# A build-time list scheduler is told that transfers land later, rotary tables load later, and the input ring grows from seven slots to eight

## The chip, the cores and the metric

The program runs on one core of a Trainium2 chip. The metric is the device time of one execution in microseconds, the median over the runs. The engines are called PE (matmul), DVE, ACT and POOL (elementwise work) and SP, which here only issues transfers. PE runs in order, and so does each other engine; they wait for each other by semaphores.

## The reference

One decoder layer on x of 1024 rows by 1024 columns, all in float32:

```
h = rmsnorm(x) * gain
p = h @ w_in                       # 1696 columns for the RWKV mixer, 1536 for attention
r, k, v, wd, ad, gd = split(token_shift_mix(p[:, :1696]))
g = sigmoid(gd) @ g_lora_up;  a = sigmoid(a0 + ad @ a_lora_up);  decay from tanh(wd) @ w_lora_up
y_rwkv = group_norm(scan of the 64x64 state of each of 8 heads) + bonus, times g
q, k, v = split(p[:, 1696:]);  rotary on the first 16 of 64 dims
y_attn = three dilated causal windows (128,1) (512,4) (2048,16), merged, normed
x = x + concat(y_rwkv, y_attn) @ w_out
gate, val = split(rmsnorm(x) @ w_ffn_up);  gate = causal conv of width 3
x = x + (silu(gate) * val) @ w_ffn_down
out = rmsnorm(x)
```

## The kernel before

Nothing in the kernel is ordered by hand. Each piece of work is handed to a scheduler that runs while the program is built (`Plan`): an op has the engines that may do it with an estimated cost on each, a rank, and the ops and buffers that it waits for. The scheduler keeps a clock of its own for each engine, takes the ready op with the best rank, and writes it down; the order in which it wrote the ops of an engine is the order in which the chip runs them. A transfer gets a `lag`, the time that its bytes take, and the scheduler holds its users back until a landing time:

```
            if eng == "SP":
                self.moved = max(self.moved, self.free[eng] + 0.6) + o.lag
                o.end = self.moved + 0.9
```

So a landing time or a lag moves no transfer by itself: it changes the moment from which a user counts as ready, and with it what is written ahead of what on every engine from there on. Nearly all transfers are issued by SP, in one queue.

The stages, with the times of the profiled execution: the first norm of x, in four groups of 256 rows (0 to 42 us); the dense input projection (to about 220 us); the RWKV mixer in 8 units (`keys`, inverses, state steps) with twelve attention column tiles at0 to at11 of the projection between them as filler for PE (220 to 490); attention heads (490 to 670); the output projection (580 to 745); the second norm (690 to 757); a Strassen-form up projection and convolution (759 to 1168); the down projection (1200 to 1404).

In the start, x comes in as 8 tiles x_0 to x_7 of 128 rows. Each is squared and summed (L370, ACT), scaled (L376, DVE), transposed in 128x128 pieces on PE (`pt_n`, L386), and copied out as a rounded high part `hT_hi` (L292 on ACT or L294 on DVE) and the rest `hT_lo` (L395, DVE). `x_n` is a ring of buffers for the x tiles and `jk_n` a ring for the squares. The gate columns `gd` and the columns `wa` of the projection are worked on as the groups come. `grow_d` (L337) writes 1024 gain values, one by one, to DRAM. `lwr` and `glr` are the two up matrices of the low-rank gates, which ACT casts to `lwh` and `gl`.

For each projected tile `in_proj` splits weights and h into two rounded parts and runs three products (L475 to L477): hi by hi, lo by hi, hi by lo. Its `cut` says in how many pieces a half of 512 rows is worked. For a unit q of the mixer, `keys` loads BK, AR and v, PE makes `pbk` (L854), `pgm` (L802) and `pv` (L839) of them, the masked products go through DRAM (`md`) into `mk`, DVE inverts 32x32 blocks (L888, L894), which come back through `mdo` into `inv`, and PE uses `inv` in `pd` (L925). In attention `kv` and `qd` read back what the tiles stored in `qkv_d`; `pav` (L1178) and `psc` (L1206) are the first products of a head. In the second norm, DVE makes `jk_n` (L1474) and PE transposes it (L1489); `a11l` (L301) is the low part of the first up-projection weights, made from the loads `rg` and `rv`.

Of the kernel before, what the change touches and what calls it, by code (L numbers as in the profile page):

```python
# [18 lines left out]
P = 128  # L19
S = 1024  # L20
D = 1024
# [58 lines left out]
class Plan:  # L80
# [70 lines left out]
    def run(self, until=None):  # L151

        until = list(until) if until is not None else None
        while any(self.todo.values()):
# [34 lines left out]
            if eng == "SP":  # L189
                self.moved = max(self.moved, self.free[eng] + 0.6) + o.lag  # L190
                o.end = self.moved + 0.9
            for u in o.users:
# [12 lines left out]
def planned_layer(ctx: ExitStack, tc: tile.TileContext, a, out):  # L205
# [14 lines left out]
    def ring(tag, n, shape, pool, dtype=F32):  # L220
        plan.ring(tag, n)
        if pool.space == PSUM:
            plan.banks.add(tag)

        def new(name):
            return plan.buf(tag, lambda: pool.tile(shape, dtype, tag=tag, name=name, bufs=n))

        return new
# [55 lines left out]
    def copy(eng, out, in_):  # L284
        if eng == ACT:
            nc.scalar.copy(out, in_)
        else:
            nc.vector.tensor_copy(out, in_)  # L288
# [38 lines left out]
    def derived():  # L327
# [8 lines left out]
        {SP: 0.5},  # L336
        lambda: nc.sync.dma_start(out=grow_d.rearrange("o (k p) -> p (o k)", p=P), in_=par[:, g_ : g_ + KD]), -150, [par_in],  # L337
        lag=1.0,
# [80 lines left out]
    with tc.tile_pool(name="xp", bufs=1) as xp:  # L419
        x_n, jk_n = ring("x", 7, [P, D], xp), ring("xjk", 1, [P, D], xp)  # L420
        for g in range(4):
# [16 lines left out]
        def in_proj(cols, name, R, evacuate, after=None, Rw=None, twice=False, cut=1):  # L438
# [16 lines left out]
            def wide():  # L455
                return raw.t[:, :, None, :r].broadcast_to([P, KD, 2, r]) if twice else raw.t[:, :, :r]

            def parted(t):
                return t[:, :, :m].rearrange("p k (x c) -> p k x c", c=r) if twice else t[:, :, :m]

            Rw = max(Rw, -279.5)
            o = chain["w"] = plan.op(COPY, lambda eng: copy(eng, parted(hi.t), wide()), Rw, ins, [raw, hi, lo])
            o2 = plan.op(
                pool(2.3), lambda: lower(POOL, parted(lo.t), wide(), parted(hi.t)), Rw, [o], [raw, hi, lo]
            )
# [77 lines left out]
        zg = tmp_n("zg")  # L543
        z_in = in_proj([(1600, GCOLS)], "gd", -198, shift_mix(13, lambda: zg.t, -198, "gd", [zg]), None, -288.5)
        gr = slice(0, GCOLS)
# [232 lines left out]
    def unit(q):  # L778
# [6 lines left out]
                b, lambda b=b: b.t.rearrange("p (f c) a t -> p f (c a t)", f=NFT),  # L785
                lambda src=src: src[:, :, q2].rearrange("f p t -> p f t"), 1.5, RB,
            )
            for b, src in ((bk, bk_d), (ar, ar_d))
        ]
        vload = load(vt, lambda: vt.t, lambda: v_d[:, :, qs].rearrange("f p t -> p f t"), 0.8, RB)  # L790

# [31 lines left out]
        def g3():  # L823
# [5 lines left out]
        stored = [  # L829
            load(gm, lambda b=b: md[b].rearrange("q s t -> s q t"), lambda b=b: g3()[blocks[b], :, blocks[b]], 0.4, RC, masked)  # L830
            for b in range(2)
# [36 lines left out]
        for rs in rss:  # L868
            o = load(mk, lambda rs=rs: mk.t[rs], lambda: md.rearrange("b q s t -> (b q) s t"), 0.4, RC, stored)
            copies.append(o)  # L870
# [29 lines left out]
        for r in range(4):  # L900
            o = plan.op(
                pool(0.06), lambda r=r: nc.gpsimd.memset(mp.t[rss[r]].rearrange("p s t -> p (s t)")[:, r : 256 : 36], 1.0),
                RC, prev, [mp],
            )
            back.append(load(mp, lambda r=r: dealt[r], lambda r=r: mp.t[rss[r]], 0.18, RC, [o]))
        inv = inv_n(f"inv{q}")
# [191 lines left out]
    for half_ in range(2):  # L1098
        tsl = slice(half_ * 512, half_ * 512 + 512)
        tabs = [rope_n(f"rope{half_}_{i}") for i in range(2)]  # L1100
        tabs_in = [
            load(tabs[i], lambda i=i, tabs=tabs: tabs[i].t, lambda i=i, tsl=tsl: a["rope"][:, i, tsl], 1.0, 200 + 5, (), tabs)
            for i in range(2)
# [811 lines left out]
```

## Time and profile before

| | us |
|---|---|
| median of 3 runs | 1426.93 (1420.82, 1426.93, 1427.86) |
| the profiled execution | 1429.69, of which its span is 1427.5 |
| PE busy | 1365.1 (96%) |
| DVE busy | 999.3 (70%) |
| ACT busy | 554.4 |
| POOL busy | 340.8 |

The span is what the trace covers; the execution's own time is 2.19 us longer. The profiled execution took 2.76 us more than the median.

### The profile page before, as it was taken

To read this page: it belongs to the slowest core of one execution; us is meant where nothing else is said; L and a number is where in the kernel's file an instruction comes from. 1 tells how busy PE (TensorE), PEld (TensorE's weight loads), DVE (VectorE), ACT (ScalarE), POOL (GpSimd) and SP (SyncE) were. 2 spreads that over 40 slices of the span, in tenths; PEclk is the share of its full clock that TensorE was granted. 3 is DMA by queue.
4 is the path that set the end of the run, shared out by engine and by line. 5 is a ranking of instruction groups with operands and counts; after the bars stand their busy time and mean duration, and the time that the engine had idled before them with its cause. 6 is when DMAs were issued, how large, how long until landed. Compare 5 with 4: busy or idle time off the path is not lost.

```text
span 1427.5 us, 21004 instructions
## 1 busy us (share of the span) xinstructions
PE 1365.1 (96%) x7872; PEld 1129.4 (79%) x7872; DVE 999.3 (70%) x2020; ACT 554.4 (39%) x957; POOL 340.8 (24%) x366
## 2 busy tenths in 40 slices
PE   5999999999999889999989999999999999999997
PEld 4788887787788777888767888888888887888886
DVE  5566663867878378988589777777777757565547
ACT  5433332133222368776245434433333434222213
POOL 4223223143453357652231000000000005111101
PEclk9999999999999989999999999999999999999999
DMA  6143437545654446522743222222222237322203
GB/s 183 45 135 119 144 111 255 155 119 161 169 148 110 105 121 188 168 85 89 247 142 102 89 89 75 74 89 86 77 89 89 78 131 248 118 89 89 89 30 118
DMA packets 172565, 173.02 MB, mean 121 GB/s; under 512 B 39632, under 2 KB 142416, under 8 KB 171440
## 3 DMA queue, kind: packets, MB, share of 16 engines
q1 hardware_dynamic: 172320, 171.16, 39.4%
q8 instruction: 62, 1.02, 0.3%
q10 hardware_dynamic: 144, 0.52, 0.1%
q14 instruction: 39, 0.32, 0.1%
HBM read 119.22 MB, written 52.43 MB: 120 GB/s over the span
## 4 chain that ended last, share of the span: by engine, by line
PE 76%; DVE 11%; DMA 7%; ACT 1%; issue 1%; POOL 1%; SPq 1%; DVEq 0%; POOLq 0%; ACTq 0%
PE c L1554 29%; PE pd L1754 5%; PE pd L1752 5%; PE pd L1753 5%; PE po L1268 2%; PE pb_at L475 2%; DVE it L888 2%; PE po L1402 2%; PE po L1403 2%; PE po L1401 2%; PE ppt L1238 1%; DVE mp L894 1%; PE pb_at L477 1%; PE pb_at L476 1%; DMA mk<-md 1%
## 5 line engine op out<-in xcount | busy, mean ns | idle before, releaser
L301 POOL TENSOR_TENSOR wl<-rw,wh 128x512 fp32r<-128x512 f32 x22 | 32.8, 1496 | 558.0 <-ACT wh L1439 544.4
L1760 DVE TENSOR_TENSOR dx<-dx,pd 128x512 f32<-128x512 f32 x128 | 85.9, 684 | 86.4 <-PE pd L1754 85.8
L1754 PE MATMUL pd<-wl,ah 128*128 128x512 f32 x352 | 138.4, 393 | 2.8 <-POOL wl L301 2.8
L1752 PE MATMUL pd<-wh,ah 128*128 128x512 f32 x352 | 138.1, 392 | 0.2 <-DVE dx L288 0.2
L1753 PE MATMUL pd<-wh,al 128*128 128x512 f32 x352 | 138.1, 392 | 0.1
L1625 DVE TENSOR_TENSOR uval<-uval,c 128x512 f32<-128x512 f32 x67 | 45.9, 685 | 62.5 <-PE c L1554 62.3
L475 PE MATMUL pb_at<-hT_hi,wh_at 128*128 128x512 f32 x192 | 82.5, 430 | 0.0
L1754 PEld LDWEIGHTS pd<-wl,ah 128*128 128x128 f32 x352 | 66.7, 190 | 17.2 <-POOL wl L301 3.2
L1752 PEld LDWEIGHTS pd<-wh,ah 128*128 128x128 f32 x352 | 66.8, 190 | 14.6 <-DVE dx L288 0.6
L1753 PEld LDWEIGHTS pd<-wh,al 128*128 128x128 f32 x352 | 66.7, 189 | 14.6 <-POOL al L301 0.5
L477 PE MATMUL pb_at<-hT_hi,wl_at 128*128 128x512 f32 x192 | 76.3, 397 | 0.0
L476 PE MATMUL pb_at<-hT_lo,wh_at 128*128 128x512 f32 x192 | 76.2, 397 | 0.0
L1656 DVE SCALAR_TENSOR_TENSOR uga<-ug,par,uga 128x1023 f32<-128x1023 f32 (+1 forms) x44 | 56.4, 1281 | 15.8 <-ACT uga L1650 15.8
L888 DVE TENSOR_TENSOR it<-mk,mp 128x60 f32<-128x60 f32 (+19 forms) x240 | 64.0, 284 | 3.3
L894 DVE TENSOR_TENSOR mp<-mp,it 128x60 f32<-128x60 f32 (+20 forms) x240 | 54.5, 244 | 3.4
L1554 PE MATMUL c<-T,s1h 128*128 128x512 f32 x176 | 55.0, 393 | 1.0 <-DVE T L1498 1.0
L1554 PE MATMUL c<-B,a11h 128*128 128x512 f32 x176 | 54.9, 392 | 0.7 <-DVE B L1498 0.5
L1554 PE MATMUL c<-B,a12h 128*128 128x512 f32 x176 | 54.7, 392 | 0.7 <-ACT uval L1629 0.7
L1554 PE MATMUL c<-T,a22h 128*128 128x512 f32 x176 | 54.8, 393 | 0.0
L1554 PE MATMUL c<-B,s4h 128*128 128x512 f32 x176 | 54.8, 393 | 0.0
L1554 PE MATMUL c<-T,s3h 128*128 128x512 f32 x176 | 54.8, 393 | 0.0
L1554 PE MATMUL c<-T,s2h 128*128 128x512 f32 x176 | 54.8, 393 | 0.0
(335 smaller groups left out, 3722.0 us busy)
## 6 DMA issues: line engine op xcount, KB each, us to landing
rg<-in_w_up SPq DMA_DIRECT2D x22, 512.0 KB
rv<-in_w_up SPq DMA_DIRECT2D x22, 512.0 KB
ra<-act_d SPq DMA_DIRECT2D x22, 512.0 KB
rw<-in_w_down SPq DMA_DIRECT2D x22, 512.0 KB
act_d<-uga SPq DMA_DIRECT2D x21, 512.0 KB
x<-in_x SPq DMA_DIRECT2D x16, 512.0 KB
wr_at<-in_w_in SPq DMA_DIRECT2D x12, 512.0 KB
qkv_d<-spl SPq DMA_DIRECT2D x24, 256.0 KB
```

Source lines behind the costliest of these rows:

```text
L475: nc.tensor.matmul(acc.t[:m, cs], hi.t[:, k, :m], hT_hi[k][:, ts_], start=(k == 0), stop=False)
L476: nc.tensor.matmul(acc.t[:m, cs], hi.t[:, k, :m], hT_lo[k][:, ts_], start=False, stop=False)
L477: nc.tensor.matmul(acc.t[:m, cs], lo.t[:, k, :m], hT_hi[k][:, ts_], start=False, stop=(k == KD - 1))
L888: nc.vector.tensor_tensor(t3(), mk.t[:, k : k + 1, k + 1 :].broadcast_to([P, r, n]), mp.t[:, 0:r, k : k + 1].broadcast_to([P, r, n]), ALU. ...
L894: nc.vector.tensor_tensor(mp.t[:, 0:r, k + 1 :], mp.t[:, 0:r, k + 1 :], t3(), ALU.add)
L1554: nc.tensor.matmul(bank.t, w.t[:, js], m, start=start and j == 0 and s, stop=j == 3 and w is lo, skip_group_check=True,)
L1625: {DVE: 0.69}, lambda: nc.vector.tensor_tensor(half_of(*out_), half_of(*x_), four(bank), ALU.add), R, after,
L1656: lambda x=x: nc.vector.scalar_tensor_tensor(ga.t[:, x:], g.t[:, : S - x], pc(f"cw{2 - x}", f), ga.t[:, x:], ALU.mult, ALU.add),
L1752: nc.tensor.matmul(pd.t, ah.t[:, ts_], wh.t, start=(j == 0), stop=False)
L1753: nc.tensor.matmul(pd.t, al.t[:, ts_], wh.t, start=False, stop=False)
L1754: nc.tensor.matmul(pd.t, ah.t[:, ts_], wl.t, start=False, stop=(j == n_ - 1))
L1760: lambda i=i, sl=sl, pd=pd: nc.vector.tensor_add(xr[i].t[:, sl], xr[i].t[:, sl], pd.t), R,
```

## The change

Seven edits. The scheduler's landing time of a transfer goes from 0.9 to 1.6 after its bytes. The lags of the mixer's transfers in short rows go up (BK and AR 1.5 to 1.9, v 0.8 to 1.2, `md` 0.4 to 0.8, `mk` 0.4 to 0.6, `mdo` 0.18 to 0.4). The store of `grow_d` gets a later rank. The x ring has eight slots and the ring of squares two. The low part of the weights of a `cut` projection may be made by POOL or DVE, where POOL alone made it. The `gd` projection is cut in two pieces of 256 rows. The rotary tables are loaded only after two attention column tiles (`cols_out[1]`).

```diff
             if eng == "SP":
                 self.moved = max(self.moved, self.free[eng] + 0.6) + o.lag
-                o.end = self.moved + 0.9
+                o.end = self.moved + 1.6
...
-        lambda: nc.sync.dma_start(out=grow_d.rearrange("o (k p) -> p (o k)", p=P), in_=par[:, g_ : g_ + KD]), -150, [par_in],
+        lambda: nc.sync.dma_start(out=grow_d.rearrange("o (k p) -> p (o k)", p=P), in_=par[:, g_ : g_ + KD]), 60, [par_in],
         lag=1.0,
...
-        x_n, jk_n = ring("x", 7, [P, D], xp), ring("xjk", 1, [P, D], xp)
+        x_n, jk_n = ring("x", 8, [P, D], xp), ring("xjk", 2, [P, D], xp)
...
+            how = LOW if cut > 1 else pool(2.3)
             o2 = plan.op(
-                pool(2.3), lambda: lower(POOL, parted(lo.t), wide(), parted(hi.t)), Rw, [o], [raw, hi, lo]
+                how, lambda *eng: lower(*(eng or (POOL,)), parted(lo.t), wide(), parted(hi.t)), Rw, [o], [raw, hi, lo]
             )
...
-        z_in = in_proj([(1600, GCOLS)], "gd", -198, shift_mix(13, lambda: zg.t, -198, "gd", [zg]), None, -288.5)
+        z_in = in_proj([(1600, GCOLS)], "gd", -198, shift_mix(13, lambda: zg.t, -198, "gd", [zg]), None, -288.5, False, 2)
...
-                lambda src=src: src[:, :, q2].rearrange("f p t -> p f t"), 1.5, RB,
+                lambda src=src: src[:, :, q2].rearrange("f p t -> p f t"), 1.9, RB,
...
-        vload = load(vt, lambda: vt.t, lambda: v_d[:, :, qs].rearrange("f p t -> p f t"), 0.8, RB)
+        vload = load(vt, lambda: vt.t, lambda: v_d[:, :, qs].rearrange("f p t -> p f t"), 1.2, RB)
...
-            load(tabs[i], lambda i=i, tabs=tabs: tabs[i].t, lambda i=i, tsl=tsl: a["rope"][:, i, tsl], 1.0, 200 + 5, (), tabs)
+            load(tabs[i], lambda i=i, tabs=tabs: tabs[i].t, lambda i=i, tsl=tsl: a["rope"][:, i, tsl], 1.0, 200 + 5, cols_out[1], tabs)
```

The diff shows what the scheduler is told; what it makes of that stands in the order of the instructions. Three places follow (a name's last number counts buffers, and is another one in the changed kernel; its line numbers from L464 on are one higher).

The first is SP's queue in the start, from the seventh x tile to the first weights of the k columns. Before:

```order
L304 DMA x_6_162<-in_x 128x1024
L304 DMA wr_gd_175<-in_w_in 128x8x96
L337 DMA grow_d_85<-par_69 128x8x1
L304 DMA x_7_235<-in_x 128x1024
L308 DMA cst2_117<-in_consts2 128x384
L304 DMA lwr_310<-in_wa_lora 128x1024
L304 DMA glr_320<-in_g_lora 96x512
L304 DMA wr_k0_527<-in_w_in 128x8x128
```

And in the changed kernel:

```order
L304 DMA x_6_162<-in_x 128x1024
L304 DMA x_7_164<-in_x 128x1024
L304 DMA wr_gd_177<-in_w_in 128x8x96
L337 DMA grow_d_85<-par_69 128x8x1
L308 DMA cst2_117<-in_consts2 128x384
L304 DMA lwr_274<-in_wa_lora 128x1024
L304 DMA glr_284<-in_g_lora 96x512
L304 DMA wr_k0_551<-in_w_in 128x8x128
```

The last x tile has moved ahead of the gate columns' weights and of `grow_d`; the rest stands as it stood, and `grow_d` still stands ahead of `cst2`, `lwr` and `glr`. On ACT, before, the square of x_7 stood between copies of the second group, and the two casts of the low-rank matrices ahead of seven of the eight copies of the third:

```order
L292 ACTIVATE hT_hi6_101<-pt_n1_1_6_302,par_69 128x256
L370 ACTIVATE jk_n1_3_1_323,ss_n1_3_1_135<-x_7_235 128x1024
L292 ACTIVATE hT_hi7_102<-pt_n1_1_7_312,par_69 128x256
L286 CAST lwh_139<-lwr_310 128x1024
L286 CAST gl_143<-glr_320 96x512
L292 ACTIVATE hT_hi1_96<-pt_n1_2_1_363,par_69 128x256
```

In the changed kernel:

```order
L292 ACTIVATE hT_hi6_101<-pt_n1_1_6_303,par_69 128x256
L292 ACTIVATE hT_hi7_102<-pt_n1_1_7_311,par_69 128x256
L286 CAST lwh_139<-lwr_274 128x1024
L286 CAST gl_143<-glr_284 96x512
L292 ACTIVATE hT_hi0_95<-pt_n1_2_0_365,par_69 128x256
L292 ACTIVATE hT_hi1_96<-pt_n1_2_1_368,par_69 128x256
```

The square of x_7 is gone from here (it stands four rows above the first one shown), and the two casts stand ahead of all eight copies of the third group.

The second place is PE at the first unit of the mixer, from the first product of its keys to `pv0`. `pb_at1_0` are filler matmuls of an attention column tile. Before (rows that only repeat are left out; a `pgm` pair has eight rows, of which the last stands here):

```order
L477 MATMUL pb_at1_0_1825<-hT_hi4_99,wl_at1_1719 128x512
L854 MATMUL pbk0_0_1857<-cst_68,BK0_1816 128x128 x4
L854 MATMUL pbk0_1_1864<-cst_68,BK0_1816 128x128 x4
L475 MATMUL pb_at1_0_1825<-hT_hi5_100,wh_at1_1718 128x512
...
L802 MATMUL pgm0_0_1_1874<-AR0_1818,BK0_1816 128x128
L839 MATMUL pv0_1885<-cst_68,v0_1823 128x128 x4
L475 MATMUL pb_at1_0_1825<-hT_hi6_101,wh_at1_1718 128x512
...
L802 MATMUL pgm0_1_1_1898<-AR0_1818,BK0_1816 128x128
```

In the changed kernel:

```order
L478 MATMUL pb_at1_0_1849<-hT_hi6_101,wl_at1_1747 128x512
L855 MATMUL pbk0_0_1880<-cst_68,BK0_1840 128x128 x4
L855 MATMUL pbk0_1_1886<-cst_68,BK0_1840 128x128 x4
L476 MATMUL pb_at1_0_1849<-hT_hi7_102,wh_at1_1746 128x512
...
L803 MATMUL pgm0_0_1_1896<-AR0_1842,BK0_1840 128x128
L476 MATMUL pb_at1_1_1910<-hT_hi0_95,wh_at1_1746 128x512
...
L803 MATMUL pgm0_1_1_1916<-AR0_1842,BK0_1840 128x128
L840 MATMUL pv0_1926<-cst_68,v0_1847 128x128 x4
```

Six filler matmuls (the pieces 5 and 6 of the tile, three each) have moved ahead of `pbk0`, and `pv0` now stands behind the second `pgm` pair and the three filler matmuls ahead of it.

The third place is PE after the last filler matmul of the last column tile, up to the first head of attention. Before:

```order
L477 MATMUL pb_at11_1_4596<-hT_hi7_102,wl_at11_4368 128x512
L960 MATMUL pzu_1776<-state1_1781,AR7_3967 128x128 x4
L969 MATMUL pzu_1776<-UV7_4056,Gm7_4060 64x64 x8
L982 MATMUL pzu_1776<-zs0_1778,Gm7_4060 64x64 x8
L992 MATMUL pzs_1777<-UV7_4056,BKt7_4042 64x64 x8
L1035 MATMUL pzu_1776<-UV7_4056,Gm7_4060 64x64 x8
L1178 MATMUL pav0_4824<-cst_68,kv0_4783 128x64 x8
```

In the changed kernel:

```order
L478 MATMUL pb_at11_1_4494<-hT_hi7_102,wl_at11_4225 128x512
L970 MATMUL pzu_1800<-UV6_3801,Gm6_3811 64x64 x8
L1072 MATMUL pyt5_4637<-cst_68,Y5_4429 128x128 x4
L983 MATMUL pzu_1800<-zs0_1802,Gm6_3811 64x64 x8
L993 MATMUL pzs_1801<-UV6_3801,BKt6_3795 64x64 x8
...
L932 MATMUL pd7_4699<-Gm7_4085,inv7_4630 32x32 x16
L983 MATMUL pzu_1800<-zs1_1803,Gm6_3811 64x64 x8
L1179 MATMUL pav0_4775<-cst_68,kv0_4692 128x64 x8
```

Ten pieces of mixer work now stand between the end of the last tile and `pav0`, where five stood; the unit in hand at that point is the seventh (q = 6), where it was the eighth.

## Rows read from the trace of the kernel before

**Rows 1.** The page: busy time by engine, and the chain that ended last.
```profile
PE 1365.1 (96%) x7872; PEld 1129.4 (79%) x7872; DVE 999.3 (70%) x2020; ACT 554.4 (39%) x957; POOL 340.8 (24%) x366
...
PE 76%; DVE 11%; DMA 7%; ACT 1%; issue 1%; POOL 1%; SPq 1%; DVEq 0%; POOLq 0%; ACTq 0%
```

**Rows 2.** Waits of PE: what for, us in total, times, longest us.
```profile
PE pt_n L386 <- DVE x L376: 10.6, 2, 7.2
...
PE pd L925 <- DVE inv L910: 4.4, 3, 3.4
PE pav L1178 <- DMA kv<-qkv_d: 3.4, 1, 3.4
...
PE pt_n L1489 <- DVE jk_n L1474: 3.1, 3, 2.2
...
PE pv L839 <- DMA v<-v_d: 1.7, 1, 1.7
...
PE pbk L854 <- DMA BK<-bk_d: 1.2, 1, 1.2
```

**Rows 3.** The chain in the start: from us, us, what.
```profile
14.98 11.82 DMA x<-in_x
```

**Rows 4.** SP's issues in the start: from us, us, what.
```profile
10.24 0.38 SPq L337 DMA_DIRECT2D grow_d<-par  x1
...
15.86 0.42 SPq L304 DMA_DIRECT2D lwr<-in_wa_lora  x1
```

**Rows 5.** Stretches of 2 us: busy by engine, clock, DMA share, GB/s.
```profile
20.00:22.00 2.00, 2.00 (x19) 2.00 (x18) 1.84 (x5) 0.71 (x2) 0.91 (x1) 1.00 0.18 33
...
26.00:28.00 2.00, 0.00 (x0) 0.00 (x0) 0.00 (x0) 1.12 (x3) 0.00 (x0) 0.50 1.08 336
```

**Rows 6.** ACT from 24 to 43: from us, us, what [idle before].
```profile
29.02 1.05 ACT L286 CAST lwh<-lwr 128x1024 fp32r<-128x1024 f32 x1 [0.63 <-DMA lwr<-in_wa_lora]
29.97 0.61 ACT L286 CAST gl<-glr 96x512 fp32r<-96x512 f32 x1
```

**Rows 7.** DVE from 24 to 43, same columns.
```profile
28.83 4.23 DVE L376 TENSOR_SCALAR x<-x,rs_n 128x1024 f32<-128x1024 f32 x3
...
34.68 4.00 DVE L395 SCALAR_TENSOR_TENSOR hT_lo<-pt_n,par,hT_hi 128x256 fp32r<-128x256 f32 x10
...
41.34 0.74 DVE L496 SCALAR_TENSOR_TENSOR zwa<-pb_wa,par,zwa 128x511 f32<-128x511 f32 x1
```

**Rows 8.** PE at 42 us, the end of the start, same columns.
```profile
42.29 0.47 PE L475 MATMUL pb_wa<-hT_hi,wh_wa 128*128 128x512 f32 x1 [1.38 <-DVE carry_wa L504]
```

**Rows 9.** Stretches of 8 us, columns as rows 5.
```profile
224.00:232.00 8.00, 5.13 (x38) 3.88 (x37) 1.29 (x2) 1.07 (x2) 4.90 (x8) 1.00 0.86 273
...
280.00:288.00 8.00, 6.76 (x71) 5.53 (x72) 5.62 (x22) 1.03 (x2) 1.31 (x1) 0.61 0.80 180
...
488.00:496.00 8.00, 3.55 (x57) 3.21 (x58) 2.17 (x4) 3.57 (x6) 5.49 (x5) 1.00 1.01 258
...
696.00:704.00 8.00, 5.78 (x30) 4.66 (x29) 5.22 (x6) 2.67 (x6) 1.94 (x4) 1.00 0.86 278
```

**Rows 10.** PE at the first unit, columns as rows 6.
```profile
225.60 0.39 PE L476 MATMUL pb_at<-hT_lo,wh_at 128*128 128x512 f32 x1
225.83 0.39 PE L477 MATMUL pb_at<-hT_hi,wl_at 128*128 128x512 f32 x1
...
229.08 1.16 PE L802 MATMUL pgm<-AR,BK 64*128 64x128 f32 x16
```

**Rows 11.** SP's issue of the rotary tables.
```profile
228.65 5.36 SPq L304 DMA_DIRECT2D rope<-in_rope  x4
```

**Rows 12.** The chain into attention.
```profile
489.00 6.16 DMA kv<-qkv_d
```

**Rows 13.** DVE at the second norm, columns as rows 6.
```profile
698.93 0.69 DVE L301 TENSOR_TENSOR a11l<-rg,a11h 128x512 fp32r<-128x512 f32 x1 [0.76 <-DMA rv<-in_w_up]
699.54 2.30 DVE L1474 SCALAR_TENSOR_TENSOR jk_n<-x,rs_n,grow 128x1024 f32<-128x1024 f32 x1
```

More of the change, by code (lines that the diff above doesn't have):

```diff
@@ L829, in unit @@
         stored = [
-            load(gm, lambda b=b: md[b].rearrange("q s t -> s q t"), lambda b=b: g3()[blocks[b], :, blocks[b]], 0.4, RC, masked)
+            load(gm, lambda b=b: md[b].rearrange("q s t -> s q t"), lambda b=b: g3()[blocks[b], :, blocks[b]], 0.8, RC, masked)
             for b in range(2)
@@ L868, in unit @@
         for rs in rss:
-            o = load(mk, lambda rs=rs: mk.t[rs], lambda: md.rearrange("b q s t -> (b q) s t"), 0.4, RC, stored)
+            o = load(mk, lambda rs=rs: mk.t[rs], lambda: md.rearrange("b q s t -> (b q) s t"), 0.6, RC, stored)
             copies.append(o)
@@ L904, in unit @@
             )
-            back.append(load(mp, lambda r=r: dealt[r], lambda r=r: mp.t[rss[r]], 0.18, RC, [o]))
+            back.append(load(mp, lambda r=r: dealt[r], lambda r=r: mp.t[rss[r]], 0.4, RC, [o]))
         inv = inv_n(f"inv{q}")
```

## The prediction

> **What bounds the kernel now.** I read the page first: PE is busy for 1365.1 of 1427.5 us, and the chain that ended last runs through PE for 76%, through DVE for 11% and through transfers for 7% [rows 1]. The change leaves PE's work as it was but for 24 longer matmuls cut in two, so it can only win or lose in the 62.4 us in which PE stands still, and where PE runs at its lower clock after standing still. The second view is therefore the list of PE's waits: 10.6 us for scaled x in the start, 4.4 for the inverses, 3.4 for the first `kv` of attention, 3.1 for the second norm, 1.7 and 1.2 for v and BK of the first unit [rows 2]. The third is each of these places by itself: the chain and the queues of the start [rows 3 to 8], and the stretches of 8 us in which PE's idle time lies [rows 9]. A place gains only where something else than the moved transfer ends the wait next, so I ask that each time.
>
> **The start.** The chain goes from x_7's issue at 14.98 for 11.82 us to its landing at 26.8 [rows 3]. It was issued late, since a ring of seven made it wait for x_0, and it then moved slowly: `grow_d`, issued at 10.24 [rows 4], was still being written in pieces of four bytes. From 20 to 22 us only 33 GB/s moved, against 336 from 26 to 28 with the store gone [rows 5]. With eight slots x_7 stands ahead of `grow_d` and should land at about 15. That takes the 4.23 us of late scaling on DVE [rows 7] out of the way. The new rank of `grow_d` does not take it out from ahead of `cst2`, `lwr` and `glr`; the order shows that it stays there.
>
> What is late next is `lwr`. Before, ACT got it at 29.02 and was through with `lwh` and `gl` 1.56 us later (29.97 plus 0.61), at 30.58 [rows 6]. After, the half megabyte of x_7 is no longer between `grow_d` and `lwr`, at 336 GB/s some 1.6 us, so that ACT is free at 29.0. Behind the two casts stand all eight copies of the third group, and then the fourth. Then 16 `hT_lo` and two `hT_hi` at 0.40 us each (4.00 for ten [rows 7]) take 7.2 us, and the shift mix and what follows it 0.95 (41.34 to PE's start at 42.29 [rows 7, 8]). Dense work starts at 29.0 + 8.15 = 37.15, against 42.29: 5.1 us earlier. I take 0.6 off, since the low-rank products now stand ahead of the first k tile and have little slack behind their sigmoid and tanh: **4.5 us gained**. The bounds: nothing, if the store holds `lwr` as long as it held x_7 and the casts end where they did with copies then waiting as before; 7.2, if `lwr` is not held at all, which is the longest of PE's waits for scaled x, gone whole [rows 2].
>
> One rule bears on what is held. By the rows, transfers behind `grow_d` crawl until it is written (33 GB/s). The Trainium skill, "DMA: Bandwidth & Descriptors", section "Queues, rings and completion order", says that descriptors are consumed in ring order on each engine, but that data descriptors carry no barrier and a later one may finish its write before an earlier one. By the second half of that rule `lwr` would land before the store is done, and the start would gain 7.2 where I say 4.5; by the row, it would not. The row decides here, as the transfer held in it was of the same size in the same queue.
>
> **The cut of gd and the low weights on DVE.** Long matmuls follow each other 0.23 us apart, and 16 of a quarter of the columns take 1.16 in all, 0.07 each [rows 10]. So two half-length ones cost 0.14 to 0.23 against 0.23; I take nothing, with an upper bound of 24 x 0.23 = 5.5 us, which would need the shorter matmul to be no shorter at all. The two low parts on DVE are worth one to three microseconds there, in the time that the late scaling leaves free.
>
> **The first unit of the mixer.** From 224 to 232 PE is busy for 5.13 of 8 us [rows 9], and the two waits, 1.2 for BK and 1.7 for v, are the whole of it [rows 2]. The scheduler now thinks that they land later, and so six filler matmuls stand ahead of `pbk0` (6 x 0.23 = 1.4, over 1.2), and 1.16 of `pgm` with three more (0.7) ahead of `pv0` (together 1.9, over 1.7) [rows 10]. **2.9 gained**, both covered by little; the bounds are 0 (the loads move later by as much) and 2.9.
>
> **The inverses.** Before, the four rotary tables keep SP busy for 5.36 us from 228.65 [rows 11], ahead of the first unit's `md` and `mk`; after, they come later, and `mk` lands sooner. Against that, the weights of at4 are now copied on DVE behind the first inversion, and `pd` of later units stands earlier in PE's order. The wait here was 4.4 in three [rows 2], and from 280 to 288 PE also ran at 0.61 of its clock [rows 9]. I take **nothing**, between 5 gained (this wait and some of the clock) and 5 lost.
>
> **Into attention.** The `kv` load takes 6.16 us from 489.00 [rows 12] and PE waits 3.4 of that [rows 2]; PE is busy for 3.55 of 8 us in this stretch [rows 9]. In the new order five more pieces of mixer work, each of 16 small matmuls at around 1 us (1.16 for a `pgm` group [rows 10]), stand between the last column tile and `pav0`: some 5 us, over 3.4. What is late next is the first `psc`, which waits for POOL's half of the keys, so I take **3 gained** with bounds of 0 and 4.45, the idle of that stretch. Inside attention DVE has little room, and I take nothing there, 4 either way.
>
> **The second norm.** `a11l` stands ahead of `jk_n` on DVE and waits for a weight load (0.76), though `jk_n` needs none of it, and PE waits 2.2 for `jk_n` [rows 2, 13]. After, `jk_n` stands ahead of `a11l`, and DVE has two splits less to do there (they went to other engines). **2 gained** of the 2.22 idle in that stretch (8 less 5.78 [rows 9]). The bounds are 0 and 2.2. The rest of the program keeps its order at the places where PE waits: nothing.
>
> **The sum** is 4.5 + 2.9 + 0 + 3 + 2 = 12.4. From the profiled execution's 1429.69 that gives 1417.3; that execution stands 2.76 above the median of the runs, 1426.93, so the forecast for the median is **1414.5**.
>
> **The rivals.** *All of the start*: `lwr` is not held, and the start gains 7.2 in place of 4.5: 1414.5 - 2.7 = **1411.8**. For it: x_7's late issue alone explains most of 26.8; against it, the 33 GB/s with x_7 waiting. *The estimates change little*: the waits at the first unit, at attention and in the second norm only move, since a load that is thought to land later is not issued sooner, and the slot freed in one place is filled by the next late thing. Only the start is left: 1426.93 - 4.5 = **1422.4**. For it: each of these waits is covered by only 0.2 us or so, and DVE is nearly full in attention. *Inverses too early in PE's order* (slower): `pd` of the third and fifth units stand 52 and 33 long matmuls earlier on PE than before, while nothing makes DVE's inverses faster. If DVE keeps its times, PE waits 52 x 0.23 + 33 x 0.23 = 19.6 us, and loses each time what it lost from 280 to 288 at a clock of 0.61, 0.39 x 8 = 3.1: 25.8 in all, against 12.4: **1440.3**. It decides from the point where the inverses lag by more than 12.4 us together. Against it: `mk` is no longer behind the rotary tables, and DVE was idle for over 2 of 8 us there [rows 9].
>
> **How the numbers follow.** My forecast gets 0.50, the whole start 0.13, the start alone 0.25, the inverses 0.12. About 0.5% (7 us) is what a measurement of this kernel can tell from no change, which makes faster anything under 1419.8 and slower anything over 1434.1. Of my forecast nine tenths lie under 1419.8, with all of the second case and a fifth of the third: 0.45 + 0.13 + 0.05 = 0.63. The same gets 0.05 + 0.20 = 0.25, slower 0.12. The forecast's own range is 1409 to 1420, from the bounds of its terms; with the cases the range reaches from 1406 (the first rival, with 5 gained at the inverses) to 1428 (the third with some new waits), which leaves out the slower case and little else.
>
> **What would show it.** Right, if in the profile of the changed kernel dense PE work starts at 36 to 39 us, x_7 lands at about 15, ACT's cast of `lwh` is what ends a wait at 27 to 28; if PE waits for neither BK nor v at 224 to 232, nor over 1 us for `kv`; and if `jk_n` of the second norm ends ahead of `a11l`. Wrong, if a wait for `inv`, `mk` or the copy of at4's weights on DVE grows past 5 us between 250 and 450, if PE's idle in attention grows, or if the start ends at 42 again because the store holds `lwr`.

## The result, and the profile after

The changed kernel takes 1408.66 us (median of four runs, 1405.70 to 1410.13) against 1426.93 us. The medians differ by 18.3 us where 12.4 was forecast. The ratio on record, formed over the runs, is 0.9883 with a 95% interval of 0.9861 to 0.9905, which is 13.6 to 19.8 us: faster, and by more than the forecast. The time lies within the range on record and 0.3 us below the forecast's own range.

The page of the changed kernel, with the rows that answer to [rows 1]:

```profile
span 1407.9 us, 21049 instructions
...
PE 1356.3 (96%) x7896; PEld 1126.9 (80%) x7896; DVE 989.6 (70%) x2021; ACT 553.5 (39%) x961; POOL 326.5 (23%) x361
...
PE 80%; DVE 9%; DMA 6%; ACT 1%; SPq 1%; issue 1%; POOL 1%; DVEq 0%; POOLq 0%; ACTq 0%
```

PE does the same work with 24 more instructions, and yet is busy for 8.8 us less. That part is the clock: matmuls that ran at the lower of its two levels (1.2 GHz, 0.50 in the rows) ran at the higher one (2.4 GHz, 1.00). So the gain is to be looked for in two sums, PE's idle time and what it lost to a low clock. I worked both out in steps of 2 us from the trace: idle is 2 less PE's busy time, and slow is the busy time by what the granted clock lacks of 1. By stage, in us of one profiled execution each (idle plus slow):

| stage | before | after | gained | forecast |
|---|---|---|---|---|
| start, to the first dense matmul | 18.0 + 2.1 | 13.8 + 1.4 | 4.9 | 4.5 |
| dense projection, to 220 | 0 | 1.5 + 0 | -1.5 | 0 |
| mixer, 220 to 470 | 10.8 + 5.0 | 7.7 + 3.4 | 4.7 | 2.9 |
| into and in attention, 470 to 580 | 13.7 + 4.8 | 9.7 + 1.6 | 7.2 | 3 |
| out projection and second norm | 9.0 + 1.5 | 8.9 + 1.5 | 0.1 | 2 |
| up projection | 0.2 + 0 | 0.9 + 0 | -0.7 | 0 |
| into the down projection | 2.9 + 2.9 | 1.3 + 0 | 4.5 | 0 |
| down projection and tail | 7.7 + 0 | 7.7 + 0 | 0 | 0 |
| sum | 78.6 | 59.4 | 19.2 | 12.4 |

The spans differ by 19.6 (1427.5 less 1407.9), so the table accounts for nearly all of it. Of the 19.2, 10.8 is idle and 8.4 is clock. The clock's part is not a chance of the two executions that were profiled: the four executions of the changed kernel were granted 0.991 to 0.993 of the clock, and 24 of the kernel before, taken for the first set of runs below, 0.980 to 0.992 with a mean of 0.986. The difference of 0.006 of 1356 us is 8 us. A single stage's clock is still that of one execution.

One border needs care. In the changed kernel a wait of 1.25 us for `s2l`, the low part of an up-projection weight, falls on the border of second norm and up projection, and 0.9 of it is counted in the latter; taken together, the two lose 11.3 us after and 10.7 before.

PE's waits in the changed kernel, columns as in [rows 2]:

```profile
PE pt_n L386 <- DVE x L376: 9.4, 2, 7.5
PE pt_n L1490 <- DVE jk_n L1475: 4.8, 3, 3.7
PE pd L926 <- DVE inv L911: 2.1, 3, 1.5
...
PE pd L1755 <- POOL wl L301: 1.3, 1, 1.3
PE psc L1207 <- POOL k L1172: 1.3, 1, 1.3
...
PE pbk L855 <- DMA BK<-bk_d: 0.9, 1, 0.9
```

`pav` no longer waits for `kv`, and `pv` no longer for v. The wait for the second norm has grown from 3.1 to 4.8.

The first of these rows has to be read with care, since the row before (10.6, with a longest of 7.2) was read wrongly in the prediction. The longest wait is the one for the very first x tile, from 0 us on, in both kernels. The wait that x_7 caused is another. Of the kernel before:

```profile
7.21 0.47 PE L386 MATMUL pt_n<-cst,x 128*128 128x128 f32 x1 [7.21 <-DVE x L376]
...
28.45 0.58 PE L475 MATMUL pb_wa<-hT_hi,wh_wa 128*128 128x256 f32 x1 [4.97 <-ACT hT_hi L292]
```

The wait of 4.97 us is gone in the changed kernel; the one for the first tile is 7.45.

The chain in the start, which answers to [rows 3, 6, 8] (from us, us, what):

```profile
15.78 12.30 DMA lwr<-in_wa_lora
28.10 1.05 ACT lwh L286
29.15 0.52 ACT gl L286
29.67 0.38 ACT hT_hi L292
...
37.69 0.47 PE pb_wa L476
```

x_7 has left the chain, and `lwr` has taken its place, 12.3 us from its issue behind the store. Its bytes were late too: the stretches of 2 us (columns as in [rows 5]) show 39 GB/s until 26 us and 274 behind it.

```profile
24.00:26.00 2.00, 2.00 (x10) 2.00 (x11) 2.00 (x6) 0.37 (x2) 0.00 (x0) 0.50 0.53 39
26.00:28.00 2.00, 2.00 (x17) 2.00 (x17) 2.00 (x4) 0.00 (x0) 0.00 (x0) 0.91 0.95 274
```

Dense work starts at 37.69, against 42.29.

Stretches of 8 us, which answer to [rows 9] (columns as in rows 5):

```profile
224.00:232.00 8.00, 8.00 (x63) 6.19 (x63) 2.57 (x4) 2.69 (x5) 2.88 (x4) 1.00 0.99 317
...
280.00:288.00 8.00, 8.00 (x62) 5.97 (x61) 7.72 (x42) 1.16 (x2) 1.62 (x5) 0.64 0.14 42
...
472.00:480.00 8.00, 6.62 (x111) 5.89 (x110) 4.89 (x10) 3.37 (x5) 5.50 (x3) 1.00 0.59 152
...
696.00:704.00 8.00, 3.62 (x21) 2.94 (x20) 6.40 (x8) 2.98 (x6) 1.18 (x3) 0.89 0.47 143
...
1176.00:1184.00 8.00, 6.76 (x30) 5.26 (x28) 7.94 (x11) 4.35 (x9) 8.00 (x7) 1.00 0.54 198
1184.00:1192.00 8.00, 7.91 (x35) 6.56 (x36) 7.51 (x8) 3.03 (x6) 7.61 (x6) 1.00 0.81 279
```

From 280 to 288 PE no longer stands still, but its clock is still low, 0.64 where it was 0.61; before that it had stood still for 1.45 us in front of the first `pd`. The last two are the same place as these two of the kernel before:

```profile
1192.00:1200.00 8.00, 6.05 (x26) 4.45 (x24) 7.76 (x11) 4.81 (x9) 8.00 (x7) 1.00 0.53 189
1200.00:1208.00 8.00, 7.05 (x19) 5.57 (x20) 4.49 (x4) 2.98 (x6) 6.93 (x6) 0.58 0.79 263
```

Before, a wait of 2.8 us for the low part of a weight tile was followed by 8 us at a clock of 0.58, which is a mix of the two levels. After, the wait there is 1.3 us and the clock stays at 1.00. This place was not in my forecast.

### The profile page after: what moved, and what is told of

Same layout as the page of the kernel before. It is cut to its first block, busy times and chain, and to the rows that moved or that the text cites. A ratio compares the mean times of both kernels' runs of the same rounds, so it can differ in the third digit from the quotient of the medians.

```text
span 1407.9 us, 21049 instructions
## 1 busy us (share of the span) xinstructions
PE 1356.3 (96%) x7896; PEld 1126.9 (80%) x7896; DVE 989.6 (70%) x2021; ACT 553.5 (39%) x961; POOL 326.5 (23%) x361
## 4 chain that ended last, share of the span: by engine, by line
PE 80%; DVE 9%; DMA 6%; ACT 1%; SPq 1%; issue 1%; POOL 1%; DVEq 0%; POOLq 0%; ACTq 0%
PE c L1555 29%; PE pd L1755 5%; PE pd L1754 5%; PE pd L1753 5%; PE po L1269 2%; PE pb_at L476 2%; PE po L1402 2%; PE ppt L1239 2%; PE po L1403 2%; PE po L1404 2%; PE pb_at L478 2%; PE pb_at L477 2%; DVE mp L895 1%; SPq L304 1%; PE pb_r L476 1%
## 5 line engine op out<-in xcount | busy, mean ns | idle before, releaser
L301 POOL TENSOR_TENSOR wl<-rw,wh 128x512 fp32r<-128x512 f32 x18 | 25.9, 1441 | 554.7 <-DVE wl L301 429.0
L1657 DVE SCALAR_TENSOR_TENSOR uga<-ug,par,uga 128x1023 f32<-128x1023 f32 (+1 forms) x44 | 56.3, 1280 | 15.8 <-ACT uga L1651 15.8
L895 DVE TENSOR_TENSOR mp<-mp,it 128x60 f32<-128x60 f32 (+23 forms) x240 | 59.4, 267 | 2.9
L889 DVE TENSOR_TENSOR it<-mk,mp 128x60 f32<-128x60 f32 (+23 forms) x240 | 54.1, 246 | 3.0
L1221 ACT ACTIVATE sm<-sm,mx 128x128 f32<-128x128 f32 (+3 forms) x64 | 49.6, 775 | 14.6 <-DVE mx L1211 14.6
```

The source lines that it names most:

```text
L889: nc.vector.tensor_tensor(t3(), mk.t[:, k : k + 1, k + 1 :].broadcast_to([P, r, n]), mp.t[:, 0:r, k : k + 1].broadcast_to([P, r, n]), ALU. ...
L895: nc.vector.tensor_tensor(mp.t[:, 0:r, k + 1 :], mp.t[:, 0:r, k + 1 :], t3(), ALU.add)
L1221: nc.scalar.activation(sm.t[:, :L], sm.t[:, :L], AF.Exp, bias=mx.t[:, x : x + 1], scale=-1.0, accum_out=den.t[:, i : i + 1])
L1657: lambda x=x: nc.vector.scalar_tensor_tensor(ga.t[:, x:], g.t[:, : S - x], pc(f"cw{2 - x}", f), ga.t[:, x:], ALU.mult, ALU.add),
```

## The experiments

The question was whether the gain is a sum of edits that each mend their own place (the first theory, "each edit its place"), or whether any edit makes the scheduler write another order, of which this one is a good one (the second, "shuffle"). "Lost" is idle plus slow, as in the table. Each ratio is against the kernel before, run on the same chip (its medians there were 1425.35, 1426.86 and 1427.30 us for the three sets of four). The first four take the two edits that I held to be the main ones, and the store.

**Eight slots alone**, on the kernel before.

```diff
-        x_n, jk_n = ring("x", 7, [P, D], xp), ring("xjk", 1, [P, D], xp)
+        x_n, jk_n = ring("x", 8, [P, D], xp), ring("xjk", 2, [P, D], xp)
```

> The kernel before with only the eight x slots and the two slots for squares. Each-edit-its-place theory: the seven-slot wait was the start's whole loss, so dense PE work starts at 37 to 39 us instead of 42.3, the waits for BK, v and kv (1.2, 1.7, 3.4 us) and the half clock at the hand-over to the down projection stay as they were, and the time is 1426.9 - 4.5 = 1422 us. Shuffle theory (any edit lets the scheduler write another order everywhere, and the gains outside the start are luck of the order): the start gains the same, but the stages behind it change by more than 3 us in one direction or the other, so the time is away from 1422 by more than 3.

1423.39 us (ratio 0.9978, 0.9956 to 1.0001). Dense work starts at 38.09. The time is the 1422 of the first theory within its noise, and the waits for BK and `kv` stayed, `kv` even longer:

```profile
PE pav L1178 <- DMA kv<-qkv_d: 4.4, 1, 4.4
```

The stages behind the start changed too, by the 3 us that the second theory asked for: the mixer lost 12.8 us (15.8 before), the second norm 14.2 (10.5). These two nearly cancel, so the time alone can't tell the theories apart.

**The landing estimate alone**, on the kernel before.

```diff
-                o.end = self.moved + 0.9
+                o.end = self.moved + 1.6
```

> The kernel before with only the landing estimate at 1.6. Each-edit-its-place theory: dense work starts at 42 us as before; the waits for BK, v and kv go, as in the changed kernel (its mixer and attention lost 12.2 us less to idle and slow clock), so about 1427 - 10 = 1417 us. Shuffle theory: the kv wait may go or stay, and the stages differ from both kernels by several us with no pattern.

1423.36 us beside 1425.35 for the kernel before; the ratio is 0.9997 (0.9972 to 1.0021), so no change. `kv` still waits 2.6, the waits for BK and v fell to 0.6 and 0.9, and the mixer (15.8 us lost) and attention (18.0) are as they were. Into the down projection it lost 1.0 us in place of 5.8. The start lost 17.8 in place of 20.1, though nothing in this edit is about the start. So the first theory is wrong on the mixer, on attention and on the start.

**The changed kernel without the landing estimate.**

```diff
-                o.end = self.moved + 1.6
+                o.end = self.moved + 0.9
```

> The changed kernel with the landing estimate back at 0.9, all else as changed. Each-edit-its-place theory: dense work still starts at about 37.7 us, but PE waits again for BK or v at the first unit (1 to 3 us) and for kv at the first head (3 us or more, with half clock behind it): 1408.7 + 8 = about 1417 us. Shuffle theory: within 3 us of 1408.7, or slower through waits at other places than these.

1424.64 us (ratio 1.0000, 0.9982 to 1.0019): the whole gain is gone, where the first theory said 1417. The chain and the stretches around the first head show where most of it went:

```profile
478.70 5.95 DMA kv<-qkv_d
484.70 1.11 PE pav L1179 x8
```

```profile
472.00:480.00 8.00, 5.34 (x78) 4.66 (x76) 0.42 (x1) 1.74 (x3) 2.19 (x3) 1.00 0.74 191
480.00:488.00 8.00, 3.30 (x42) 3.12 (x43) 5.80 (x8) 1.94 (x3) 4.54 (x4) 0.64 0.77 145
488.00:496.00 8.00, 7.29 (x70) 6.62 (x70) 0.98 (x3) 3.59 (x7) 7.32 (x6) 0.50 0.30 69
```

PE stands still for 5.3 us at `pav` and then runs at 0.64 and 0.50 of its clock. Attention lost 19.8 us in all (11.3 in the changed kernel), the second norm 13.1 (10.4), and the way into the down projection 4.2 (1.3).

**The store behind the low-rank matrices.**

```diff
-    grow_out = plan.op({SP: 0.5}, ..., 60, [par_in], lag=1.0)
...
         o = load(glr, lambda: glr.t[gr, 0:RW], lambda: a["g_lora"], 0.6, -183, x_last)
+        grow_out = plan.op({SP: 0.5}, ..., 60, [par_raw, o], lag=1.0)
```

> The changed kernel with the store of the gains issued behind the two low-rank matrices (it waits for the second to land) and not ahead of them. Held-transfer theory: lwr, which landed 12.3 us after its issue behind the store, lands within 4 us of its issue, by 18 us; ACT's copies of the third group are no longer behind it, dense work starts at 33 to 35 us instead of 37.7, and the time is 1408.7 - 3 = 1405 to 1406 us. DVE-bound theory: DVE has so much to do from 8 to 37 us that the start ends at 37 anyway, and the time is 1408 to 1409 us.

1408.84 us (ratio 0.9892, 0.9862 to 0.9922), the changed kernel's time. Dense work starts at 35.86, between the two theories. The chain there is now DVE's:

```profile
24.75 3.58 DVE x L372 x3
28.33 4.70 DVE hT_lo L391 x12
```

ACT had `lwh` at 21.90 without a wait for `lwr`; when `lwr` landed can't be seen. So the store held the start by 1.8 us and no more, and DVE bounds what is left. The 1.8 us didn't reach the end: attention lost 15.0 us here, against 11.3.

The next four take away the other edits of the changed kernel one by one, and put two of them together on the kernel before.

**The changed kernel without the tables' wait.**

```diff
-... 1.0, 200 + 5, cols_out[1], tabs)
+... 1.0, 200 + 5, (), tabs)
```

> The changed kernel with the rotary tables loaded without the wait for two column tiles, as before. Each-edit-its-place theory: the tables again keep SP for 5.4 us ahead of the first unit's stores and loads, so the first inversions end later, PE's idle and slow clock between 220 and 470 us goes up from 11.1 to 14 or 15, the rest stays, and the time is 1408.7 + 4 = 1413 us. Shuffle theory: another order everywhere; the hand-over into attention (11.3 us lost in the changed kernel) is worse by several us and the time is 1415 or more, or nothing changes.

1430.13 us (ratio 1.0027, 1.0010 to 1.0044): slower than the kernel before, though it has six of the seven edits. SP's queue, PE's waits, one row of DVE and one of PE:

```profile
227.68 5.57 SPq L304 DMA_DIRECT2D rope<-in_rope  x4
...
246.76 1.84 SPq L304 DMA_DIRECT2D mk<-md  x4
```

```profile
PE pd L926 <- DVE inv L911: 9.8, 3, 6.2
```

```profile
279.23 0.69 DVE L1117 TENSOR_TENSOR x_rot<-x_rot,rope 128x512 f32<-128x512 f32 x1 [2.62 <-DMA x_rot<-qkv_d]
...
287.89 1.91 PE L926 MATMUL pd<-inv,Gm 32*32 32x32 f32 x32 [6.21 <-DVE inv L911]
```

The stretches there:

```profile
280.00:288.00 8.00, 1.79 (x10) 1.17 (x9) 7.54 (x35) 1.53 (x2) 2.26 (x2) 0.77 0.97 234
288.00:296.00 8.00, 7.33 (x78) 6.10 (x79) 6.64 (x14) 1.15 (x2) 4.06 (x6) 0.50 0.61 173
```

The tables stand ahead of the first unit's stores, and the first `mk` is issued at 246.76 where the changed kernel issues it at 238.91. DVE's inversion starts 7.6 us later for it (254.28 against 246.73), and then DVE stands still for 2.6 us in front of a rotary product that stands ahead of the rest of the inversion in its order and whose input has not landed. PE stands still for 6.2 of 8 us at `pd` and then runs at 0.50 of its clock. The mixer loses 25.2 us, against 11.1, and attention 20.9, against 11.3. PE is not early here: it comes to the first `pd` at 281.68 (287.89 less 6.21), where the kernel before came to it at 277.80.

**The changed kernel without the longer lags** (the five numbers of the diff in one line).

```diff
-  1.9, RB,  ...  1.2, RB)  ...  0.8, RC, masked)  ...  0.6, RC, stored)  ...  0.4, RC, [o])
+  1.5, RB,  ...  0.8, RB)  ...  0.4, RC, masked)  ...  0.4, RC, stored)  ...  0.18, RC, [o])
```

> The changed kernel with the lags of the mixer's transfers as before. Each-edit-its-place theory: the longer lags are what puts filler matmuls of the column tiles earlier, so that the last tile ended 21 us earlier than before (464 against 485 us, of which the start is 4.6). Without them it ends at about 475 us, and PE waits for kv again (2 to 4 us), so about 1408.7 + 5 = 1414 us. Shuffle theory: the last tile ends where it did, within 3 us, and the time is within 3 of 1408.7.

1418.71 us (ratio 0.9951, 0.9935 to 0.9968); the profiled execution took 1412.53, the lowest of five. The last column tile ended at 464.7, so the lags don't move it, and the mechanism that I gave for them is wrong; but the time is 10 us longer. Hardly any of it is idle: the profiled execution has 52.6 us of idle in all, against 51.6 in the changed kernel. The profile's loss is in attention: 18.4 us, of which 6.5 is clock. The five executions go with their granted clock, from 1412.53 us at 0.990 to 1421.69 at 0.984, where the changed kernel had 0.991 to 0.993. Why the clock of one kernel differs that much from execution to execution is not shown.

**The changed kernel with the gate columns uncut and the low parts on POOL.**

```diff
-            how = LOW if cut > 1 else pool(2.3)
+            how = pool(2.3)
...
-... None, -288.5, False, 2)
+... None, -288.5)
```

> The changed kernel with the gate columns uncut and the low parts of the cut weights on POOL, as before. Each-edit-its-place theory: these two cost and give nothing but what they do in the start, so dense work starts within 1 us of 37.7 and the time is 1408 to 1410 us. Rival: the cut is part of the start's gain, and dense work starts at 39 us or later; 1411 us.

1408.86 us (ratio 0.9875, 0.9858 to 0.9892). Dense work starts at 38.02. These two edits give nothing. The seventh edit, the later rank of the store, was not taken away by itself.

**Slots and landing estimate together, on the kernel before.**

```diff
-        x_n, jk_n = ring("x", 7, [P, D], xp), ring("xjk", 1, [P, D], xp)
+        x_n, jk_n = ring("x", 8, [P, D], xp), ring("xjk", 2, [P, D], xp)
...
-                o.end = self.moved + 0.9
+                o.end = self.moved + 1.6
```

> The kernel before with the eight slots and the landing estimate at 1.6, none of the other edits. If the edits add up, the start is that of the slots alone (16.0 us lost against 20.1), and the weights of the down projection come in time as with the estimate alone (1.0 lost against 5.8), while the mixer and the hand-over into attention stay bad (33 us lost together, against 22 in the changed kernel): 1425.4 - 4 - 5 = 1416 us. If what counts is the whole set (the lags and the tables too), it stays at 1420 or more; if the landing estimate and the slots are all of it, 1409.

1421.73 us (ratio 0.9962, 0.9945 to 0.9980). The start (14.5 us lost) and the way into the down projection (0.8) are mended, as a sum of the two would have it; the mixer is not, with 22.9 us lost. These two edits are not all of the gain.

The last four ask about the tables, and about two versions that might be better.

**The tables' wait alone**, on the kernel before.

```diff
-... 1.0, 200 + 5, (), tabs)
+... 1.0, 200 + 5, cols_out[1], tabs)
```

> The kernel before with only the rotary tables' wait for two column tiles. Undoing this edit in the changed kernel cost 21 us (1430 against 1409), by inverses that came later than PE asked for them. If the tables cost that much wherever they stand, this kernel gains most of it: 1410 us or less. If the tables cost much only together with the other edits, which put the reading of the inverses earlier on PE: the first inverse ends some 4 us earlier (276 to 277 us against 280.5), PE's 3.4 us wait for it and the half clock behind it go, the mixer loses 10 us in place of 15.8, the hand-over into attention stays bad, and the time is 1426 - 6 = 1420 us.

1425.97 us (ratio 0.9988, 0.9966 to 1.0010): nothing. The first inverse came at 277.08 where it was 280.48, as expected, but its wait hardly fell (3.1 where it was 3.4), since PE came to it at 274.75 where it was 277.80, and a new wait came up:

```profile
PE pyt L1071 <- POOL Y L1062: 5.0, 1, 5.0
...
PE pav L1178 <- DMA kv<-qkv_d: 4.4, 1, 4.4
PE pd L925 <- DVE inv L910: 3.6, 2, 3.1
```

**Slots, landing estimate and tables** on the kernel before; to the two edits of the kernel with slots and estimate this adds:

```diff
-... 1.0, 200 + 5, (), tabs)
+... 1.0, 200 + 5, cols_out[1], tabs)
```

> The kernel before with three edits: eight slots, the landing estimate at 1.6, and the tables' wait; lags, gate columns and the store of the gains as before. If these three are what the change is worth, the mixer loses 11 us as in the changed kernel (22.9 with the first two alone), attention about 11, and the time is 1409 to 1411 us. If the longer lags are needed too (without them the changed kernel took 1418.7), it is 1417 to 1420.

1414.92 us (ratio 0.9925, 0.9901 to 0.9949), between the two. The mixer loses 10.4 us in place of 22.9: the same edit that gave nothing alone gives 12.5 us in that stage here. Attention loses 22.2, of which 10.6 is clock, in a profiled execution that took 1419.27, above its median.

**The tables later still**, in the changed kernel with the gate columns uncut.

```diff
-... 200 + 5, cols_out[1], tabs)
+... 200 + 5, cols_out[2], tabs)
```

> The changed kernel with the gate columns uncut (1408.9 that way) and the tables' wait moved from the second to the third column tile. If the tables still stood in the way of the second unit's stores and loads, the mixer's loss goes from 9 us to 6 or 7 and the time is 1405 to 1407. If they did not: 1408 to 1410, or some us more if the first rotary products now wait for them.

1412.76 us (ratio 0.9908, 0.9876 to 0.9940): not better. PE waits 6.1 us for one inverse, which came at 282.60.

**A landing estimate of 2.0**, in the changed kernel with the gate columns uncut.

```diff
-                o.end = self.moved + 1.6
+                o.end = self.moved + 2.0
```

> The changed kernel with the gate columns uncut and the landing estimate at 2.0 in place of 1.6. If the estimate works by covering waits for transfers, those left (BK 0.9, and the first weights of the down projection 1.3 in the changed kernel) go, and the time is 1405 to 1408. If it is only another order: anywhere from 1405 to 1425, with new waits at places that have no transfer in them.

1433.46 us (ratio 1.0043, 1.0018 to 1.0068), the highest median of all, though its interval overlaps that of the kernel without the tables' wait. Three of its four longest waits behind the start:

```profile
PE po L1403 <- DVE yl L301: 7.4, 3, 3.7
PE c L1555 <- ACT T L1497: 3.2, 1, 3.2
PE psc L1207 <- POOL k L1172: 2.8, 1, 2.8
```

They wait for DVE, ACT and POOL, not for a transfer; what held those three was not followed. What was worked out as idle and slow came to 18.9 us in the second norm, against 10.4.

No version beat the changed kernel.

## Why the prediction was right, step by step

**The start** was right in mechanism and size, though a slip is covered by luck. In the changed kernel the casts were done at 29.67, where I had 29.0: `lwr` came only 0.9 us earlier than before (28.10 against 29.02), where I had 1.6. The work behind the casts took 8.0 us, where I had 8.15, so dense work began at 37.69, where the sum gave 37.15. The 0.6 that I had taken off for the low-rank products happens to cover that; what those cost was a wait of 0.4 later on, in the dense projection. Alone, eight slots moved the start to 38.09 and the time by 0.22%, whose interval just reaches no change. The rival that the store doesn't hold `lwr` fell: it landed 12.3 us after its issue, while the copies waited for it. The rule of the Trainium skill, "DMA: Bandwidth & Descriptors", section "Queues, rings and completion order", that a later descriptor may finish its write ahead of an earlier one, is not what this trace shows for `lwr`, whose bytes moved late as well. That descriptors are consumed in ring order, as the same section says, agrees with the trace. The rule says may, not will, so it did not ask for the early landing that the prediction took from it.

The price of that rival, 7.2, was a misreading: it is PE's wait for the first x tile, which no edit here touches. What x_7 cost PE was the wait of 4.97 us. With the store out of the way DVE gave 35.86, a gain of 6.4, which is the bound that the runs show.

**The first unit** was right: PE is busy for 8.00 of 8 us where it was 5.13, a gain of 2.9. The next BK then waits 0.9.

**The inverses**, taken at nothing, gave 1.8 (4.7 of the mixer less 2.9): the waits for them fell from 4.4 to 2.1 us. That small number rests on one edit. Without the tables' wait the mixer loses 14.1 us more than the changed kernel (25.2 less 11.1) and 9.4 more than the kernel before, far beyond the bounds of 5 that I gave. The argument that I set against the slower rival, that `mk` is no longer behind the tables, is what decided. The rival's own mechanism is not what the runs show. It had PE come to the third and fifth `pd` too early. In the changed kernel these do run 13 and 10 us earlier (318.92 and 388.91, against 332.04 and 398.57), and wait for an inverse by 0 and 0.3 us. In the kernel without the tables' wait PE waits for the first, fourth and seventh inverse, not for the third or fifth, and at the first it is later than before, not earlier: there DVE is late, through `mk` and through the rotary product in its order.

**Into attention** was right in mechanism and mis-sized: 3 was forecast and 7.2 came. The wait of 3.4 for `kv` is gone, and the first `psc` waits 1.3 for POOL's keys, as the step says, which leaves 2.1 of the 3. What the step left out is the clock (slow fell by 3.2) and waits inside attention, which it took at nothing: idle fell by 4.0 in all, so 1.9 of it lies there. Part of the 7.2 is luck, since all but one of the other kernels with the same landing estimate lose 15 to 22 us in this stage.

**The second norm** was the step that failed. The order turned as I said, `jk_n` no longer stands behind `a11l`, but its longest wait grew from 2.2 to 3.7 and its waits together from 3.1 to 4.8. So the term of 2 gained was 1.7 lost. The stage shows 0.1 gained only because another wait, which I had not counted, fell: the out projection's for `yl`, from 2.8 to 0.7. The row that I took for the cause, the load ahead of `jk_n` on DVE, was not what ends the wait next. In the changed kernel the chain there is:

```profile
695.82 1.70 DVE jk_n L1475
697.52 0.61 DVE x L1414
...
698.15 1.15 ACT jk_n L1469 x2
699.30 0.48 ACT B L1497
...
699.80 0.52 DVE B L1499
...
700.41 0.68 DVE B L1499
701.09 1.20 DVE jk_n L1475
```

With the load out of the way, one tile of x after the other goes through DVE, the square on ACT and back to DVE, and two additions of the up projection (`B`) stand ahead of the last `jk_n` on DVE. What that `jk_n` reads was ready at 700.21, when POOL ended `rs_n`, so the additions held it by 0.9 us; the rest is the chain itself.

**Into the down projection** I had nothing, and 4.5 came: the low part of the weights there was late by 2.8 us and is late by 1.3, and the 2.9 us of clock lost behind the wait are gone. The sentence of the prediction that the rest of the program keeps its order where PE waits was wrong here. This goes with the landing estimate: the four kernels with 0.9 lose 5.8, 3.6, 4.2 and 4.5 us at this place, and of the nine with 1.6 eight lose 0.2 to 1.3 and one 2.8. That a longer estimate of landing makes the scheduler write these splits earlier fits with it, but was not followed in the order.

**The sum** came out too small by 6 us, and the reason is clock that I had not priced. The idle alone gained 10.8, less than the 12.4 that I had; the clock gave 8.4, where my sum has nothing. What a wait costs behind it is uneven. In the kernel before, the 2.8 us for `wl` were followed by 3.0 us of lost clock, the 3.4 for `kv` by 1.5, and the 2.2 for `jk_n` by none:

```profile
496.00:504.00 8.00, 7.33 (x68) 6.49 (x68) 5.12 (x16) 3.07 (x8) 2.99 (x3) 0.79 0.69 165
...
704.00:712.00 8.00, 8.00 (x40) 6.62 (x40) 7.27 (x10) 4.76 (x11) 2.57 (x4) 1.00 0.66 221
```

In sum that kernel has 16.3 us of slow beside 62.3 of idle, where I had counted the idle alone.

On the rivals: "the estimates change little" fell, since undoing the landing estimate takes back all of the gain. But the theory that each edit mends its place fell too. Alone, the slots, the estimate and the tables give 0.2%, nothing and nothing; the first two give 0.4% together, the three 0.75%, all seven 1.2%. Taking away the estimate or the tables loses everything, and the lags about half. The gain is one of the set, and that much is shown. How the edits need each other is shown in one place only, the tables and the first inverses; for the estimate and the lags the cause stays open. What stays open too is why the stage into attention comes out so differently (11 to 22 us lost among the kernels with 1.6), and with it how much of the best order is luck; a landing estimate of 2.0, further in the same direction, has the highest median of all, so it is not a matter of more cover.

## What to carry to other kernels

In a kernel whose order comes out of estimates at build time, an edit of an estimate has no price of its own: test it with the edits around it undone and done, since the same edit gave 0 us in one set and 20 in another. When a wait of the bounding engine is priced, add what its clock loses behind the wait, from a stretch of the same trace at that very place, since it ran from nothing to 3 us here. Look up when a wait happens before giving it a cause: a list of waits has no times. Ahead of a forecast on "this instruction no longer stands behind that one", look for the next thing that the reader waits for; where it is a chain through a busy engine, the gain can be nothing, as in the second norm.

## What the hardware showed that I had not expected

A transfer that stands ahead of the slow store in SP's queue may land late too. The gate columns' weights were issued at 7.93 in the changed kernel, 2.9 us ahead of the store, and ACT waited for them until 22.07:

```profile
22.07 0.83 ACT L286 CAST wh_gd<-wr_gd 128x768 fp32r<-128x768 f32 x1 [3.32 <-DMA wr_gd<-in_w_in]
```

In the kernel before, issued at 5.97 and 4.3 us ahead of the store, they were there by 18.06. With the store behind `glr`, issued 0.49 us after it, `glr` came 11.3 us after its issue, though hardly a byte moved from 20 to 24 us:

```profile
23.80 0.62 ACT L286 CAST gl<-glr 96x512 fp32r<-96x512 f32 x1 [0.86 <-DMA glr<-in_g_lora]
```

```profile
20.00:22.00 2.00, 1.64 (x14) 1.37 (x12) 2.00 (x5) 1.75 (x5) 0.00 (x0) 1.00 0.00 0
22.00:24.00 2.00, 1.62 (x14) 1.55 (x14) 2.00 (x6) 1.14 (x2) 0.98 (x1) 1.00 0.01 3
```

Both are the last transfer ahead of the store. In nine of the kernels with eight slots the store is issued some 2.9 us behind the gate columns' weights, and ACT waits for these until 12.7 to 14.8 us after their issue; in a tenth (the tables later still) they were there within 11.8. With the store behind `glr` they were there by 18.13, at most 10.4 us after their issue at 7.71. That speaks for the store, but one kernel is no proof of it: whether the store holds back their completion, or some other thing does, stays open.
